# An opening by quarters, a rope ahead of a sum, and matmuls that nobody reads

## The chip, the core and the metric

The kernel runs on one core of one Trainium2 chip. The metric is the device time of one execution in microseconds (us), the median of several runs. Weights stream from HBM into SBUF by DMA, TensorE multiplies, VectorE (DVE), ScalarE (ACT) and GpSimd (POOL) do the rest, and SyncE (SP) issues nearly all transfers.

## The reference

Two layers, 256 tokens, 1024 features, everything in float32. Each layer mixes tokens (attention with 8 heads in one block of 256, beside a pooling mixer) and then applies a mixture of 16 experts, of which each token uses two. `plain` below is a layer norm without gain and bias, `LN` one with them.

```
cond = silu(c)
for l in 0, 1:
    sh1, sc1, g1, sh2, sc2, g2 = split(cond @ w_mod[l] + b_mod[l], 6)
    h = plain(x) * (1 + sc1) + sh1
    q, k, v, p = split(h @ w_in[l])               # 512 columns each
    a = attention(rope(q), rope(k), v)            # causal, softmax
    m = pool_mixer(p) @ w_pool[l] * pool_scale[l]
    x = LN1(alpha * x + g1 * (concat(a, m) @ w_out[l]))
    h = plain(x) * (1 + sc2) + sh2
    gates = top2_of_one_group(softmax(h @ w_router))
    y = sum_e gates[e] * (silu(h @ w_gate[e]) * (h @ w_up[e])) @ w_down[e]
    x = LN2(alpha * x + g2 * y)
```

## The kernel before

**The stream.** All weights, 265 MiB, come through one list of transfers, mostly of 1 MiB, in the order in which they are needed (`Stream`). SP issues the next one as soon as fewer than `limit` tiles are live; a tile is freed in the code behind its last matmul or VectorE operation, and the transfer that takes over its slot waits for that. The ring has 21 slots, some of which also serve as scratch; `st.allow` changes the limit between the stages.

**The order of the work.** Each engine runs its instructions in the order in which the code emits them, so a wait holds all that is emitted behind it on that engine. Nothing is reordered by a planner.

**The opening (layer 0).** `load_x` brings x in two halves of 128 tokens. `add_mod01(h)` lists the modulation weights of shift and scale for half h of the features (512): four tiles with rows of 512 columns, which are runs of 2 KB. `mod01(h)` multiplies them by the condition, `mod01_fin(h)` transposes the resulting row into columns and adds the bias. `enter` transposes the normalised x (L416) and applies scale and shift on its way to `hT`; `qk_mm` multiplies `hT` by the weights of queries and keys (L434), by feature blocks, for 128 tokens t at a time. The order is: half 0 of the features, its query and key matmuls for both t, half 1, its matmuls.

**The mixer.** `mod_dve(l, v, acc)` computes a modulation row on VectorE as a running sum of eight multiplies (L356, L358): v = 2 is the gate g1, 4 the scale sc2, 3 the shift sh2. `rope` turns queries and keys in place by twelve small VectorE operations (L709 to L714). `qT` and `kT` are transposes of them (L501), copied out by VectorE (queries) and ScalarE (keys) at L502; L508 and L513 are the scores. `pool` runs on GpSimd (L718 to L727). Before the change `mod_dve(l, 2)` stands ahead of `rope` in both layers.

**The router and the gather.** `exps`, `gate` and `router` rank the experts by a chain of small VectorE operations that ends in the mask `r_M`; five tiny matmuls with triangular and all-one matrices count the tokens of each expert (L784 to L789); `onehot` compares the result with slot numbers (L821), and `gather` copies the tokens into expert slots by matmuls with those one-hot matrices (L843).

**The experts.** Eight pairs a layer, each pair side by side in the halves of the array: `gate_up` (L885), `silu` (L899 to L902), `act_t` (four transposes, L908, and a copy, L910), `down` (L922), `combine` (L947). In layer 0 `mod_fin(1, 1)` stands behind the first pair's gate and up matmuls.

**Between the layers and at the end.** The last pair's results stay in PSUM. `experts` returns mean and power of the variance for both halves of the tokens, and the norms are applied by `norm` at the start of the next layer or at the end of the kernel, where `norm_aside` puts one quarter of it on ScalarE and GpSimd.

Of the kernel before, what the change touches and what calls it, by code (L numbers as in the profile page):

```python
# [16 lines left out]
D = 1024  # L17
# [56 lines left out]
def tile_trunk(ctx, tc, x, c, w_mod, b_mod, w_in, w_pool, pool_scale, w_out, ln1_g, ln1_b,  # L74
# [30 lines left out]
    def add_mod01(h):  # L105

        w = w_mod[0].rearrange("(p k) n -> p k n", k=8)
        for q in range(2):
            for v in range(2):
                st.add(("m01", h, q, v), w[:, 4 * q:4 * q + 4, v * D + h * 512:v * D + (h + 1) * 512])  # L110
# [42 lines left out]
    for h in range(2):  # L153
        add_mod01(h)
        if not h:
            load_x(1)
        add_qk(0, 2 * h)
        add_qk(0, 2 * h + 1)
# [46 lines left out]
    small_loads()  # L205
# [38 lines left out]

    pscol = const.tile([128, 8], F, name="pscol")
# [34 lines left out]

    colt = {}
# [31 lines left out]

    def mod01_fin(h, acc):
        part = s2()
        A.copy(part, acc)
        b = ps()
        for k in range(4):
            T.transpose(b[:, k * 128:(k + 1) * 128], part[:, k * 128:(k + 1) * 128], ident)
        o = col01[:, :, 4 * h:4 * h + 4]  # L320
        V.reduce_sum(o, b.rearrange("p (k v o r) -> p v k o r", k=4, v=2, o=2)[:, :, :, :, 0], axis=AX.X)
        V.tensor_add(o, o, bcol[:, 0, 4 * h:4 * h + 4, 0:2].rearrange("p k v -> p v k"))
# [58 lines left out]
    def stats_end(b):  # L381
        mv = tiny.tile([128, 2], F, name="mv")
        V.bn_aggr(mv, b)
        rs = tiny.tile([128, 1], F, name="rs")
# [25 lines left out]
    def enter(l, t, hT, xn, hs=(0, 1)):  # L410

        for h in hs:
# [12 lines left out]
    def mixer(l, hT, xn, ready):  # L425
        pq = [[ps(), ps()] for _ in range(2)]

        def qk_mm(t, qs=range(4)):
            for q in qs:
                w = st.get(("in", l, "qk", q))  # L430
                for kk in range(2):
# [4 lines left out]
                if t:  # L436
# [6 lines left out]
        else:  # L443

            ready(0)
            for t in range(2):
                qk_mm(t, (0, 1))
            ready(1)
            qk_mm(0, (2, 3))
        st.allow(NS - 6)  # L450
        qk = big.tile([128, 2, D], F, name="xn")
        for t in range(2):
            if t:
                qk_mm(1, range(4) if l else (2, 3))
# [6 lines left out]
        mod_dve(l, 2, acc[2])  # L461
        if l:
            mod_dve(l, 4, acc[4])
        rope(qk)

# [226 lines left out]
        exps(0)  # L692

# [50 lines left out]
    def router(l, mes, gate):  # L744
# [4 lines left out]
        gate()  # L749
# [409 lines left out]
```

## Time and profile before

| what | value |
|---|---|
| runs | 731.86 us median of 3 (729.12 to 734.01) |
| profiled execution | 732.26 us; span from first to last instruction 730.5 us |
| mean granted TensorE clock | 0.977 of full |
| busy share of the span | TensorE 92%, VectorE 44%, ScalarE 17%, GpSimd 6% |
| moved by DMA | 280.36 MB, mean 384 GB/s |

How to read it: busy time is the union of an engine's instructions over the span. The granted clock has two levels, 1.2 and 2.4 GHz; 0.5 in a window means the lower one throughout. The profile's rows name a line of the kernel and what it writes and reads: `ps` is a PSUM bank, `wr` a slot of the ring, `s` a scratch tile of 512 columns.

### The profile page before, as it was taken

How to read it: one execution, taken by the hardware profiler on the slowest of the kernel's cores; microseconds unless marked ns; L12 is line 12 of the kernel's file. 1: busy time of each engine (PE TensorE's matmuls, PEld its weight loads, DVE VectorE, ACT ScalarE, POOL GpSimd, SP SyncE). 2: the span in 40 equal slices, each digit the busy share in tenths (PEclk: the TensorE clock that was granted, in tenths of full speed). 3: DMA queues.
4: the chain of work that ended last, by engine and by line, in shares of the span. 5: the costliest groups of instructions: out<-in, count | busy, mean ns of one | idle time of the engine just before them, and what ended most of it. 6: DMA issues, size and time to landing. Idle time of an engine off the chain costs nothing. (4 is left out here: it accounts for less than half of the span.)

```text
span 730.5 us, 8092 instructions
## 1 busy us (share of the span) xinstructions
PE 675.4 (92%) x3101; PEld 322.0 (44%) x3101; DVE 323.9 (44%) x572; ACT 127.7 (17%) x274; POOL 46.9 (6%) x74
## 2 busy tenths in 40 slices
PE   4899799979899999999979999997999999998994
PEld 1347455544333363333324575555434345332331
DVE  2117898652243343232253876665332342342315
ACT  0111332122001121101102125213210111111100
POOL 4000500100000000000000041010000000000001
PEclk9999899999999999999999999997999999999998
DMA  9999999798999999999999999967599999999992
GB/s 325 395 391 408 410 370 379 282 415 323 423 422 419 421 421 423 421 417 418 398 408 390 409 410 415 372 266 309 216 423 421 422 421 421 421 418 421 418 399 91
DMA packets 57633, 280.36 MB, mean 384 GB/s; under 512 B 5009, under 2 KB 6073, under 8 KB 34537
## 3 DMA queue, kind: packets, MB, share of 16 engines
q1 hardware_dynamic: 56944, 279.20, 94.8%
q8 instruction: 29, 0.48, 0.3%
q10 hardware_dynamic: 312, 0.32, 0.1%
q0 software_dynamic: 320, 0.14, 0.1%
q14 instruction: 28, 0.22, 0.1%
HBM read 278.59 MB, written 1.05 MB: 383 GB/s over the span
## 5 line engine op out<-in xcount | busy, mean ns | idle before, releaser
L885 PE MATMUL ps<-wr 128*64 128x512 f32 x1024 | 224.3, 593 | 0.0
L885 PEld LDWEIGHTS ps<-wr 128*64 128x64 f32 x1024 | 73.1, 137 | 145.6 <-issue 140.7
L922 PE MATMUL ps<-wr,s 128*64 128x512 f32 x512 | 115.3, 602 | 4.0 <-ACT s L910 4.0
L922 PEld LDWEIGHTS ps<-wr,s 128*64 128x64 f32 x512 | 36.1, 138 | 73.3 <-issue 64.0
L932 DVE SCALAR_TENSOR_TENSOR s<-ps,gc,gb 128x512 f32<-128x512 f32 x32 | 23.9, 748 | 89.0 <-PE ps L922 89.0
L434 PE MATMUL ps<-wr,hT 128*128 128x512 f32 x128 | 56.9, 603 | 0.9 <-ACT hT L423 0.6
L596 PE MATMUL ps<-wr,hT 128*128 128x512 f32 (+1 forms) x160 | 55.7, 507 | 0.0
L358 DVE SCALAR_TENSOR_TENSOR wr<-wr,condT 128x1024 f32<-128x1024 f32 x42 | 54.2, 1290 | 2.3 <-DMA wr<-in_w_mod_dram 0.8
L935 ACT CAST wr<-s 128x512 fp32r<-128x512 f32 x30 | 18.5, 618 | 167.1 <-PE ps L885 109.1
L902 DVE TENSOR_TENSOR s<-s,ps 128x512 f32<-128x512 f32 x16 | 11.0, 687 | 79.4 <-PE ps L885 79.4
L936 DVE TENSOR_TENSOR wr<-s,wr 128x512 fp32r<-128x512 f32 x30 | 20.8, 692 | 55.6 <-ACT wr L935 50.8
L596 PEld LDWEIGHTS ps<-wr,hT 128*128 128x128 f32 x160 | 30.2, 190 | 23.8 <-issue 21.3
L434 PEld LDWEIGHTS ps<-wr,hT 128*128 128x128 f32 x128 | 24.4, 194 | 31.0 <-issue 28.5
L947 PE MATMUL ps<-wr,sT 128*128 128x512 f32 x120 | 33.6, 412 | 0.0
L910 ACT COPY s<-ps 128x512 f32<-128x512 f32 x16 | 9.4, 587 | 135.4 <-PE ps L908 135.4
L843 PE MATMUL ps<-s,xn 128*128 128x512 f32 x64 | 28.9, 451 | 2.1 <-DVE s L821 2.1
L1085 POOL TENSOR_TENSOR rs<-rs,mhalf 128x2 f32<-128x2 f32 x2 | 1.4, 702 | 457.1 <-DVE rs L1084 457.1
L552 PE MATMUL ps<-wr,hT 128*128 128x512 f32 x64 | 28.3, 596 | 0.0
L947 PEld LDWEIGHTS ps<-wr,sT 128*128 128x128 f32 x120 | 20.9, 189 | 16.3 <-issue 13.0
L478 PE MATMUL ps<-hT,wr 128*128 128x256 f32 x128 | 28.1, 380 | 0.0
L843 PE MATMUL ps<-s,hT 128*128 128x512 f32 x64 | 27.6, 431 | 0.0
L478 PEld LDWEIGHTS ps<-hT,wr 128*128 128x128 f32 x128 | 24.2, 190 | 4.5 <-issue 1.3
(236 smaller groups left out, 627.2 us busy)
## 6 DMA issues: line engine op xcount, KB each, us to landing
wr<-in_w_gate_dram SPq DMA_DIRECT2D x64, 1024.0 KB, 18.2
wr<-in_w_up_dram SPq DMA_DIRECT2D x60, 1024.0 KB, 18.8
wr<-in_w_down_dram SPq DMA_DIRECT2D x56, 1024.0 KB, 18.7
wr<-in_w_mod_dram SPq DMA_DIRECT2D x48, 1024.0 KB, 14.6
wr<-in_w_in_dram SPq DMA_DIRECT2D x16, 1024.0 KB, 16.7
wr<-in_w_out_dram SPq DMA_DIRECT2D x8, 1024.0 KB, 18.6
wr<-in_w_down_dram SPq DMA_DIRECT2D x12, 512.0 KB, 11.1
wr<-in_w_up_dram SPq DMA_DIRECT2D x8, 512.0 KB, 17.4
```

Of the source, the lines that this page charges most:

```text
L358: V.scalar_tensor_tensor(acc, w[:, kk], condT[:, k, 0:1], acc, op0=OP.mult, op1=OP.add)
L434: T.matmul(pq[t][n], hT[:, k, t * 128:(t + 1) * 128], w[:, kk, n * 512:(n + 1) * 512], start=(k == 0), stop=(k == 7))
L478: T.matmul(pp[g // 2][:, (g % 2) * 256:(g % 2) * 256 + 256], w[:, kk, g * 128:(g + 1) * 128], hT[:, k, :], start=(k == 0 and g % 2 == 0), ...
L552: T.matmul(pv[t], hT[:, k, t * 128:(t + 1) * 128], w[:, kk, :], start=(k == 0), stop=(k == 7))
L596: T.matmul(py[t][-1][:, 0:c1 - c0], catT[:, k, t * 128:(t + 1) * 128], w[:, kk, n * 512 + c0:n * 512 + c1], start=(q == 2 and kk == 0), st ...
L843: T.matmul(b, xs[:, t, k::8], SX[i][t], start=(n == 0), stop=(n == 3))
L885: T.matmul(bs[nm][64 * j:64 * j + 64, :], XE[i][k // 4][:, k % 4, c0:c0 + 64], st.get((nm, l, 2 * i + j, q))[:, k - k0, :], start=(k == 0) ...
L922: T.matmul(bo[n][64 * j:64 * j + 64, :], AT[i][:, k, 64 * j:64 * j + 64], st.get(("d", l, 2 * i + j, q))[:, k - k0, (n - n0) * 512:(n - n0 ...
L932: V.scalar_tensor_tensor(o, bo[n], GC[i], g2[:, c0], op0=OP.mult, op1=OP.mult)
L935: A.copy(oh[:, c0], o)
L936: V.tensor_sub(ol[:, c0], o, oh[:, c0].bitcast(F))
L947: T.matmul(b, STt[i][:, t * 128:(t + 1) * 128], o[:, n * 512:(n + 1) * 512], start=(start and j == 0), stop=(stop and j == 1), skip_group_ ...
```

## The change

- The opening goes by quarters of 256 features: two modulation tiles each (shift and scale, rows of 256 columns, runs of 1 KB), then one tile of query and key weights. `mod01`, `mod01_fin` and the new `enter01` handle a quarter; while a quarter's row is being turned into columns, TensorE multiplies the previous quarter's remaining blocks.
- The small loads on GpSimd's queue are issued behind the constants.
- In layer 0 the rope comes ahead of `mod_dve(0, 2)`.
- `warm(n)` multiplies an all-one matrix n times into a PSUM bank that nobody reads: 10, 2 and 3 times in the opening, 3 and 8 at the start of layer 1, 7 behind the first `exps` of layer 1, 6 behind `gate` and 4 behind the counts in both layers.
- `mod_fin(1, 1)` moves from expert pair 0 to pair 1 of layer 0; `act_t` splits its copy between VectorE and ScalarE in the first and last pair.
- The statistics of the second half of the tokens move behind the first half's norm work (`ends(t)`); three buffers instead of two for mean and power.

```diff
-        for q in range(2):
-            for v in range(2):
-                st.add(("m01", h, q, v), w[:, 4 * q:4 * q + 4, v * D + h * 512:v * D + (h + 1) * 512])
+        for v in (1, 0):
+            st.add(("m01", h, v), w[:, :, v * D + h * 256:v * D + (h + 1) * 256])
...
-    for h in range(2):
+    for h in range(4):
         add_mod01(h)
         if not h:
             load_x(1)
-        add_qk(0, 2 * h)
-        add_qk(0, 2 * h + 1)
+        add_qk(0, h)
...
     V.tensor_mul(condT[:, :, 0], th, cc)
-    small_loads()
     wr = const.tile([128, 8, 32], F, name="wr_")
...
     V.reciprocal(rcnt, rcnt)
 
+    small_loads()
...
+    def warm(n):
+
+        b = ps().rearrange("p (a c) -> p a c", a=4)
+        for _ in range(n):
+            T.matmul(b, ones, ones[:, None, :].to_broadcast([128, 4, 128]), start=True, stop=True)
...
     def mod01(h):
 
         acc = ps()
-        for q in range(2):
-            for kk in range(4):
-                for v in range(2):
-                    j = 2 * v + kk % 2
-                    T.matmul(acc[32 * j:32 * j + 32, :], condT[:, 4 * q + kk, :], st.get(("m01", h, q, v))[:, kk, :],
-                             start=(q == 0 and kk < 2), stop=(q == 1 and kk > 1))
+        for k in range(8):
             for v in range(2):
-                st.free(("m01", h, q, v))
-        return acc
-
-    def mod01_fin(h, acc):
-        part = s2()
-        A.copy(part, acc)
+                j = 2 * v + k % 2
+                T.matmul(acc[32 * j:32 * j + 32, 0:256], condT[:, k, :], st.get(("m01", h, v))[:, k, :],
+                         start=(k < 2), stop=(k > 5))
+        for v in range(2):
+            st.free(("m01", h, v))
+        part = s2(256)
+        A.copy(part, acc[:, 0:256])
+        return part
...
-        mv = tiny.tile([128, 2], F, name="mv")
+        mv = tiny.tile([128, 2], F, name="mv", bufs=3)
...
+    def enter01(h, hT, xn):
+
+        b = ps()
+        for k in range(2):
+            for t in range(2):
+                T.transpose(b[:, k * S + t * 128:k * S + (t + 1) * 128],
+                            xn[:, t, (2 * h + k) * 128:(2 * h + k + 1) * 128], ident)
+        return b
+
+    def enter01_fin(h, hT, b):
+        for k in range(2):
+            kk = 2 * h + k
+            o, i = hT[:, kk, :], b[:, k * S:(k + 1) * S]
+            if k:
+                V.tensor_scalar(o, i, colt[0, 1][:, kk:kk + 1], colt[0, 0][:, kk:kk + 1], op0=OP.mult, op1=OP.add)
+            else:
+                A.activation(o, i, AF.Identity, scale=colt[0, 1][:, kk:kk + 1], bias=colt[0, 0][:, kk:kk + 1])
...
-            ready(0)
-            for t in range(2):
-                qk_mm(t, (0, 1))
-            ready(1)
-            qk_mm(0, (2, 3))
+            for q in range(4):
+                if not q:
+                    ready(0)()
+                qk_mm(0, (q,))
+                if q < 3:
+                    fin = ready(q + 1, lambda: qk_mm(1, (q,), (0,)))
+                    qk_mm(1, (q,), (1,))
+                    fin()
...
-        mod_dve(l, 2, acc[2])
         if l:
+            mod_dve(l, 2, acc[2])
             mod_dve(l, 4, acc[4])
         rope(qk)
+        if not l:
+            mod_dve(l, 2, acc[2])
...
         exps(0)
+        if l + 1 == DEPTH:
+            warm(7)
...
         gate()
+        warm(6)
...
         T.matmul(pc[:, 0:16], ones, M[:, 1], start=False, stop=True)
+        warm(4)
...
-            A.copy(a, b.rearrange("p (k s) -> p k s", k=4))
+            bv = b.rearrange("p (k s) -> p k s", k=4)
+            if i in (0, NPAIR - 1):
+                V.tensor_copy(a[:, 0:2], bv[:, 0:2])
+                A.copy(a[:, 2:4], bv[:, 2:4])
+            else:
+                A.copy(a, bv)
...
-                    V.bn_stats(bn[t][:, 1, :], XB[t][1])
...
-                if l + 1 < DEPTH:
-                    mod_fin(l + 1, 1)
...
+            if i == 1 and l + 1 < DEPTH:
+                mod_fin(l + 1, 1)
...
-        mv2 = tiny.tile([128, 2, 2], F, name="mv2", bufs=1)
-        rs2 = tiny.tile([128, 2], F, name="rs2", bufs=1)
-        for t in range(2):
-            V.bn_aggr(mv2[:, t], bn[t])
-        V.tensor_scalar_add(rs2, mv2[:, :, 1], EPS)
-        P.tensor_tensor(rs2, rs2, mhalf.to_broadcast([128, 2]), op=OP.pow)
-        return [(mv2[:, t], rs2[:, t:t + 1]) for t in range(2)], norm, norm_aside
+        def ends(t):
+            V.bn_stats(bn[t][:, 1, :], XB[t][1])
+            return stats_end(bn[t])
+
+        return ends, norm, norm_aside
...
+            warm(10)
             bias_cols()
 
-            def ready(h):
-                mod01_fin(h, mod01(h))
-                for t in range(2):
-                    enter(0, t, hT, xn, (h,))
+            def ready(h, between=lambda: None):
+                part = mod01(h)
+                if not h:
+                    warm(2)
+                between()
+                mod01_fin(h, part)
+                b = enter01(h, hT, xn)
+                if not h:
+                    warm(3)
+                return lambda: enter01_fin(h, hT, b)
         else:
             mod_mm(l, 0)
+            warm(3)
...
                 b = tiny.tile([128, 2, 6], F, name="bn")
+                if not t:
+                    own.append(ends(0))
...
-                V.tensor_scalar(xn[:, t], xt[:, t], mv[:, 0:1], rs, op0=OP.subtract, op1=OP.mult)
                 if not t:
                     mod_fin(l, 0)
+                    warm(8)
+                    own.append(ends(1))
+                V.tensor_scalar(xn[:, t], xt[:, t], mv[:, 0:1], rs, op0=OP.subtract, op1=OP.mult)
                 enter(l, t, hT, xn)
...
+    def second():
+        own[1] = ends(1)
+        norm_aside(1, 512, D, rest, *own[1])
```

## Rows read from the trace of the kernel before

In the windows the columns are: stretch, its length, busy time and instructions of the engines, the granted clock, DMA share, GB/s. In a timeline they are: start, duration, engine, line, operation, tiles, count, and in brackets the idle time before and what ended it.

**Rows 1.** Windows: DMA rate in five stretches.
```profile
41.00:50.00 9.00, 8.41 (x28) 4.44 (x29) 1.86 (x7) 2.46 (x6) 0.00 (x0) 1.00 1.05 380
250.00:300.00 50.00, 50.00 (x232) 24.12 (x230) 16.88 (x27) 6.13 (x9) 0.00 (x0) 1.00 1.01 421
90.00:180.00 90.00, 84.80 (x440) 47.76 (x440) 59.43 (x101) 25.16 (x52) 5.15 (x5) 0.98 0.89 353
470.00:522.00 52.00, 47.62 (x271) 29.81 (x271) 31.51 (x71) 13.84 (x26) 4.08 (x4) 0.90 0.62 243
522.00:716.00 194.00, 189.11 (x874) 76.07 (x871) 60.38 (x101) 23.82 (x39) 0.00 (x0) 1.00 1.00 413
```

**Rows 2.** Waits of TensorE: us in total, times, longest.
```profile
PE ps L501 <- DVE xn L714: 5.7, 2, 4.2
...
PE ps L908 <- DVE s L902: 3.6, 4, 1.8
PE ps L784 <- DVE r_M L778: 2.8, 2, 2.3
PE ps L843 <- DVE s L821: 2.1, 2, 1.0
PE ps L624 <- DVE wr L391: 1.9, 1, 1.9
...
PE ps L293 <- DMA wr<-in_w_mod_dram: 1.2, 1, 1.2
```

**Rows 3.** Timeline of the opening.
```profile
18.16 1.28 DVE L378 BATCH_NORM_STATS2 bn<-xt 128x6 f32<-128x512 f32 x2 [3.31 <-DMA xt<-in_x_dram]
...
23.14 14.00 PE L434 MATMUL ps<-wr,hT 128*128 128x512 f32 x32 [0.65 <-ACT hT L423]
...
37.07 3.64 PE L308 MATMUL ps<-wr,condT 128*32 128x512 f32 x32
...
41.94 1.04 PE L416 MATMUL ps<-ident,xn 128*128 128x128 f32 x8
...
43.12 14.00 PE L434 MATMUL ps<-wr,hT 128*128 128x512 f32 x32
```

**Rows 4.** Timeline from the gate's sum to the scores, layer 0.
```profile
62.98 9.21 DVE L358 SCALAR_TENSOR_TENSOR wr<-wr,condT 128x1024 f32<-128x1024 f32 x7
...
73.47 2.11 POOL L718 TENSOR_TENSOR wr<-wr 128x1084 f32<-128x1084 f32 x1 [1.03 <-DMA wr<-in_w_mod_dram]
...
73.64 2.08 DVE L710 TENSOR_TENSOR s<-xn,cs 128x128 f32<-128x128 f32 x1
...
80.83 2.08 PE L508 MATMUL ps<-wr 64*128 64x128 f32 x16
```

**Rows 5.** Timeline of the tail, VectorE.
```profile
721.47 0.74 DVE L1067 SCALAR_TENSOR_TENSOR xt<-ps,mv,wr 128x512 f32<-128x512 f32 x1
```

**Rows 6.** Windows: stretches at the lower clock.
```profile
76.20:83.00 6.80, 4.04 (x26) 3.75 (x28) 3.87 (x5) 0.59 (x1) 6.39 (x12) 0.50 1.03 410
158.20:161.60 3.40, 3.40 (x8) 2.80 (x9) 0.36 (x1) 0.78 (x1) 0.00 (x0) 0.51 1.00 422
...
383.40:386.80 3.40, 3.40 (x11) 2.27 (x11) 3.29 (x6) 2.52 (x8) 0.00 (x0) 0.50 1.03 408
496.10:502.90 6.80, 6.22 (x29) 2.96 (x28) 4.97 (x15) 2.49 (x6) 0.00 (x0) 0.50 1.01 418
506.30:509.70 3.40, 3.40 (x9) 2.81 (x9) 0.81 (x1) 0.78 (x1) 0.00 (x0) 0.50 0.18 75
```

**Rows 7.** Timeline of layer 1's router, VectorE.
```profile
499.61 0.17 DVE L684 TENSOR_REDUCE r_mx<-ps 128x1 f32<-128x16 f32 x1 [1.05 <-PE ps L683]
```

**Rows 8.** Timeline of the passage to layer 1.
```profile
375.56 0.70 DVE L943 BATCH_NORM_STATS2 bnx<-ps 128x6 f32<-128x512 f32 x1 [0.16 <-PE ps L942]
...
381.20 0.66 PE L332 MATMUL ps<-ident,s 128*128 128x128 f32 x4 [0.71 <-ACT s L327]
...
382.33 0.81 DVE L1112 TENSOR_SCALAR xn<-xt,mv,rs 128x1024 f32<-128x1024 f32 x1 [0.73 <-POOL rs L386]
```

More of the change, by code (lines that the diff above doesn't have):

```diff
@@ L303, in mod01, with mod01_fin @@
         acc = ps()
-        for q in range(2):
-            for kk in range(4):
-                for v in range(2):
-                    j = 2 * v + kk % 2
-                    T.matmul(acc[32 * j:32 * j + 32, :], condT[:, 4 * q + kk, :], st.get(("m01", h, q, v))[:, kk, :],
-                             start=(q == 0 and kk < 2), stop=(q == 1 and kk > 1))
-            for v in range(2):
-                st.free(("m01", h, q, v))
-        return acc
-    def mod01_fin(h, acc):
-        part = s2()
-        A.copy(part, acc)
+        for k in range(8):
+            for v in range(2):
+                j = 2 * v + k % 2
[6 more added lines that the diff above has]
+        return part
+    def mod01_fin(h, part):
         b = ps()
-        for k in range(4):
+        for k in range(2):
             T.transpose(b[:, k * 128:(k + 1) * 128], part[:, k * 128:(k + 1) * 128], ident)
-        o = col01[:, :, 4 * h:4 * h + 4]
-        V.reduce_sum(o, b.rearrange("p (k v o r) -> p v k o r", k=4, v=2, o=2)[:, :, :, :, 0], axis=AX.X)
-        V.tensor_add(o, o, bcol[:, 0, 4 * h:4 * h + 4, 0:2].rearrange("p k v -> p v k"))
+        o = col01[:, :, 2 * h:2 * h + 2]
+        V.reduce_sum(o, b[:, 0:256].rearrange("p (k v o r) -> p v k o r", k=2, v=2, o=2)[:, :, :, :, 0], axis=AX.X)
+        V.tensor_add(o, o, bcol[:, 0, 2 * h:2 * h + 2, 0:2].rearrange("p k v -> p v k"))
     def mod_fin(l, v):
@@ L381, in stats_end @@
     def stats_end(b):
-        mv = tiny.tile([128, 2], F, name="mv")
+        mv = tiny.tile([128, 2], F, name="mv", bufs=3)
         V.bn_aggr(mv, b)
-        rs = tiny.tile([128, 1], F, name="rs")
+        rs = tiny.tile([128, 1], F, name="rs", bufs=3)
         V.tensor_scalar_add(rs, mv[:, 1:2], EPS)
@@ L407, in norm_rows, with enter @@
         return ts
-    def enter(l, t, hT, xn, hs=(0, 1)):
-        for h in hs:
+    def enter01(h, hT, xn):
[6 more added lines that the diff above has]
+    def enter01_fin(h, hT, b):
+        for k in range(2):
+            kk = 2 * h + k
[4 more added lines that the diff above has]
+                A.activation(o, i, AF.Identity, scale=colt[0, 1][:, kk:kk + 1], bias=colt[0, 0][:, kk:kk + 1])
+    def enter(l, t, hT, xn):
+        for h in range(2):
             b = ps()
@@ L426, in mixer, with qk_mm @@
         pq = [[ps(), ps()] for _ in range(2)]
-        def qk_mm(t, qs=range(4)):
+        def qk_mm(t, qs=range(4), kks=range(2)):
             for q in qs:
                 w = st.get(("in", l, "qk", q))
-                for kk in range(2):
+                for kk in kks:
                     for n in range(2):
@@ L435, in qk_mm @@
                                  start=(k == 0), stop=(k == 7))
-                if t:
+                if t and 1 in kks:
                     st.free(("in", l, "qk", q))
@@ L453, in mixer @@
             if t:
-                qk_mm(1, range(4) if l else (2, 3))
+                qk_mm(1, range(4) if l else (3,))
             A.activation(qk[:, t, 0:512], pq[t][0], AF.Copy, scale=DH ** -0.5)
@@ L1119, in tile_trunk @@
     rest = xt[:, 1, 512:D]
+    own = [ends(0), None]
+    def second():
+        own[1] = ends(1)
+        norm_aside(1, 512, D, rest, *own[1])
     for t, a, b in ((0, 0, 512), (0, 512, D), (1, 0, 512)):
-        norm(t, a, b, xt[:, t, a:b], *ends[t], (lambda: norm_aside(1, 512, D, rest, *ends[1])) if t == a == 0 else None)
+        norm(t, a, b, xt[:, t, a:b], *own[t], second if t == a == 0 else None)
         nc.sync.dma_start(out[0, t * 128:(t + 1) * 128, a:b], xt[:, t, a:b])
```

3 lines of the change are left out of this document (2 added, 1 removed).

## The prediction

> **What bounds the kernel now.** I read first the windows of DMA traffic by stage, then who waited for whom on TensorE, then the windows where the granted clock falls, and last the timelines of the places that the change touches. All times are of the profiled execution, 732.26 us with a span of 730.5; the median of the three runs, 731.86, lies 0.4 lower.
>
> The weight stream and TensorE bound this kernel in turns, tied by the ring of slots. The reader is to see this in [rows 1]. With 8 KB runs and no gap the stream moves 421 GB/s (stretch 250 to 300). From 90 to 180 it moves 353, so (421 - 353) / 421 x 90 = 14.5 us of it are lost, because slots come free only as the mixer, the router and the first expert pair use their weights. From 470 to 522 it moves 243: 22 us lost in the same way in layer 1. From 522 to 716 it runs at 413 almost unbroken while TensorE is busy 189 of 194 us; TensorE starts those experts with a full ring and ends with an empty one. So what TensorE saves inside the expert pairs is taken back by the stream, seen at the end of layer 0 as the 1.2 us that L293 waits for its last modulation tile [rows 2]. What TensorE and VectorE save ahead of the first expert pair lets slots go, and the stream run, earlier by as much, up to the lost time of that layer. I therefore count savings ahead of 167 us (layer 0) and between 380 and 515 us (layer 1), and the tail, and nothing else.
>
> **The change part by part.**
>
> *Opening.* The queries' and keys' matmuls start at 23.14, 4.98 after the second half of x arrives at 18.16 [rows 3]. Ahead of it stood x's first half and four tiles (4.2 MB) of modulation weights; now two (2.1 MB), which at 380 GB/s [rows 1] is 5.5 us sooner. The tiles now have rows of 1 KB, which no row here shows. Per engine of the 16, a 2 KB packet takes 2048 x 16 / 380 = 86 ns and an 8 KB one 8192 x 16 / 421 = 311 ns, so 37 ns per KB and 12 ns for each packet; 1 KB would take 49 ns, 334 GB/s (estimate), 0.4 us more per tile. The bounds are no loss (86 / 2 = 43 ns) and a packet that costs 86 ns whatever its size (190 GB/s); I take 49, for the line passes through both sizes. So the start moves to 23.14 - 5.5 + 0.8 = 18.4. From there TensorE does 28.0 of query and key matmuls (two times 14.00), three modulation quarters at half of 3.64 (5.5), and three times six transposes at 1.04 / 8 (2.3) [rows 3]: 35.8, ending at 54.2 where it ended at 57.1. The copy and reduction behind each quarter lie under 1.75 us of matmuls that the change places between them; without that cover they would cost 1 us a quarter, the bound on this side. A quarter's 3.15 MB take 8.9 us of stream against 9.6 of TensorE, so data just keep up. Gain 3.0, between 0 and 5. The ten first filling matmuls, the small loads moved on GpSimd's queue behind the constants, and the bias transposes lie ahead of x's arrival: nothing, as long as GpSimd's nine issues, now ahead of the statistics' power, end before x's second half is in; if not, some 1 us. The third buffer of the statistics costs nothing.
>
> *Rope ahead of the gate's modulation sum (layer 0).* TensorE waits 5.7 us in two waits for the rope [rows 2]. It stands behind the sum's eight multiplies, which run to 62.98 + 9.21 = 72.19; of its twelve operations the first seven take 1.5 us, up to 73.64, and the next was held up for 2.08 beside GpSimd's addition [rows 4]. Now the rope runs before GpSimd starts, in some 2.7 us, and the sum ends at 74.9 in the old time. Its four slots come free 2.7 later, and the three matmuls of the gate's rows that need it stay behind it; the ring is not short of slots before 90. The wait is not gone: the query copies on VectorE now stand behind the sum, and the score matmuls behind them. With a copy like the 0.74 of a 128x512 operation [rows 5] they start at 75.6 where they started at 80.83: 5.2. If the last multiply (9.21 / 7 = 1.3) must wait for the addition that ends at 73.47 + 2.11 = 75.58 [rows 4], they start at 77.6: 3.2. In addition the clock ran at half speed from 76.2 to 83.0, with TensorE busy 4.04 [rows 6], so up to 2.0 come back if the shorter wait leaves it high. I take 5.0 for the whole, between 3.2 and 7.1.
>
> *Filling matmuls in the routers.* Each has 512 columns in one pass, as a gather's matmul has, of which eight took 3.40 at half clock: 0.43, or 0.21 at full [rows 6]. Layer 0 has six in a wait of 2.3 and four in one of 1.05, layer 1 seven in 1.9, six and four [rows 2]; at full clock 1.3, 0.9 and 1.5, so they fit and cost nothing; at half clock they would overrun by 0.3, 0.7 and 1.1. In layer 1 the six stand in a wait of only 0.5, but the stretch before it ran at half clock and shortens. What they can give is the clock. The gathers' first 3.4 us ran at half speed in both layers, after TensorE had stood idle on VectorE's ranks: 1.7 each. In layer 1 it was at half speed from 496.1 to 502.9 too, after the 1.9 us wait: there VectorE waited 1.05 for the second logits [rows 7] and would start that much sooner. 1.7 in layer 0 and 2.7 in layer 1, and a loss of 1 in each layer if the clock falls all the same.
>
> *Between the layers.* Of the statistics, one bn_stats (0.70) and an aggregation leave the way to the first half. But the second half's now stand between the shift's reduction and the normalisation xn, which ended at 383.14. The reduction waits for transposes of the modulation row, which end at 381.86; some 0.4 for it, 0.70 and two small operations (0.3) for the statistics, and 0.81 for xn make 384.1 [rows 8]: 1.0 later. The eleven fills lie in that wait; they may save the half clock from 383.4 to 386.8 (1.7, [rows 6]). I take 0, between -1.0 and +0.7.
>
> *Within the experts.* Moving the mod_fin from pair 0 to pair 1 and halving act_t's copy shorten the 3.6 us of waits at L908 [rows 2] and the copies behind them; at pair 1 TensorE then waits some 1.2 for the moved copy, which stands behind act_t's on ScalarE. All of it is spent against the stream: 0 (the moved accumulator holds a PSUM bank longer, also 0).
>
> *Tail.* The second half's statistics now follow the first normalisation operation (0.74, [rows 5]), less one aggregation: 0.6 later.
>
> Sum: 3.0 + 5.0 + 1.7 = 9.7 in layer 0, under the stream's 14.5 - 3.0 (eight tiles x 0.4) = 11.5; 0 between the layers; 2.7 in layer 1, far under 22; -0.6: 11.8. From 732.26 that is 720.5, on the median's scale 720.
>
> **Rivals.**
>
> *The clock falls all the same.* Then 1.7, 2.7 and the rope's 1 to 2 are missing: 731.9 - (3.0 + 4.0 - 0.6) = 725.5. For it: the fills are short and much around them in the routers are transposes and matmuls of 32 columns. Against it: the waits that they fill are just those after which it fell. The Trainium skill, "TensorE: Matmul & The Clock Gate", section "Part 4: PE-mode transpose", says that transposes don't lift the clock, since they do not count as busy in the same way; no row here separates them, and by it this rival is what happens in layer 1's router, where sixteen follow the fills.
>
> *The rope's wait comes back whole.* If GpSimd's additions (2.11 and those after) get in between VectorE's last two multiplies, the scores start at 79 or later and only 1 is left: 731.9 - (3.0 + 1.0 + 1.7 + 2.7 - 0.6) = 724. The held-up operation of 2.08 beside an addition of 2.11 speaks for it [rows 4]; that seven of the eight multiplies end before the addition starts speaks against it. The Trainium skill, "VectorE: DVE Perf Modes", section "Two Vector instructions with no wait between them", calls the interface through which VectorE reads a second SBUF operand shared with GpSimd; the multiply, too, reads two, and by that rule the 3.2 above is the price and not the 5.2.
>
> *Slower: the 1 KB packets bound the opening.* If a packet costs 86 ns whatever its size, two tiles take 11 us, a quarter 13.7, and the last quarter's matmuls end near 72 where they ended at 57: 15 lost, of which 8.8 come back later (5.0 + 1.7 + 2.7 - 0.6), so 738. It decides below about 300 GB/s, where a quarter's data take longer than its TensorE work, and turns the whole slower at about 220. The rates at 2 and 8 KB speak against it, for there the price follows the size.
>
> *More is set free.* The opening gives 5, the rope 7.1, and layer 0 reaches the stream's 11.5: with 2.7 and 0.7 that is 717.5.
>
> **How the numbers follow.** The forecast 0.53, the clock 0.19, the rope 0.13, more 0.09, slower 0.06. The range goes from 717.5 less the runs' own spread (2.7 below the median) to the clock rival with the low opening and rope, 731.9 - (0 + 3.2 - 0.6) = 729.3: 715 to 729. Faster by over 1% means below 724.5, and 1% (7.3 us) is about what a measurement of runs from 729.12 to 734.01 tells from none: the forecast, "more", half of the rope's and a little of the clock's, 0.73. Within 1%: 0.21. Slower: 0.06.
>
> **What would show it.** Right: scores' first matmul near 73 instead of 80.83; query and key matmuls from 18 to 54; full clock in both gathers; 353 and 243 GB/s both higher; L293's wait for its tile kept or longer; VectorE's chain at the end longer by 0.6. Wrong: TensorE waiting for DMA inside the opening, fills that delay the matmul behind them, VectorE's multiplies of the sum over 1.3 us beside GpSimd, or an expert stage of layer 1 that does not end earlier though it starts earlier.

## The result, and the profile after

The changed kernel takes 724.39 us, median of eight runs (721.74 to 726.67), beside 731.44 for the kernel before: a ratio of 0.990 (95% interval 0.9875 to 0.9924), a gain of 7.05 us where 11.8 were forecast. Measured a second time it took 724.16 beside 733.32: 0.9885 (0.9860 to 0.9911). Its profiled execution took 721.74 with a span of 719.9, 10.5 under the span of before. It happens to be the fastest of the eight: its mean granted clock was 0.991, that of the other seven 0.986 to 0.989. So the next paragraphs compare two single executions, and what separates them from the medians is a question for the experiments.

The stretches of the execution, as windows (columns as in [rows 1]):

```profile
22.00:55.00 33.00, 32.99 (x173) 15.50 (x173) 2.77 (x10) 5.24 (x11) 0.00 (x0) 1.00 1.06 376
85.00:175.00 90.00, 87.33 (x460) 48.83 (x460) 59.49 (x101) 23.18 (x47) 5.21 (x5) 1.00 0.99 400
460.00:511.00 51.00, 48.25 (x297) 30.37 (x298) 32.55 (x72) 14.37 (x27) 4.14 (x4) 1.00 0.67 262
511.00:705.00 194.00, 188.62 (x873) 76.40 (x870) 61.16 (x103) 23.38 (x39) 0.00 (x0) 1.00 1.00 413
...
75.60:79.00 3.40, 3.40 (x20) 2.77 (x16) 3.04 (x6) 1.64 (x10) 3.24 (x7) 0.50 1.03 408
151.50:155.00 3.50, 3.43 (x13) 3.46 (x14) 1.33 (x2) 0.82 (x2) 0.00 (x0) 1.00 1.02 431
321.30:324.70 3.40, 3.40 (x10) 0.98 (x8) 0.69 (x1) 1.80 (x4) 0.00 (x0) 0.50 1.02 410
...
495.60:499.00 3.40, 3.33 (x13) 3.36 (x14) 1.33 (x2) 0.78 (x1) 0.00 (x0) 1.00 0.67 282
```

Beside [rows 1] the stream from the scores to the first expert pair rose from 353 to 400 GB/s, that of layer 1's router from 243 to 262, and the expert stage of layer 1 is what it was: 413 over 194 us. Beside [rows 6] both gathers (151.5 and 495.6) now run at the full clock. What is left at the lower one, up to the last matmuls, is one stretch at the scores, and one inside layer 0's experts, now at 321.3.

The places that the change touches, as a timeline (columns as in [rows 3]):

```profile
16.67 0.55 PE L418 MATMUL ps<-ident,xn 128*128 128x128 f32 x3 [1.37 <-DVE xn L394]
18.06 3.70 PE L455 MATMUL ps<-wr,hT 128*128 128x512 f32 x8 [0.20 <-ACT hT L429]
22.01 1.29 PE L311 MATMUL ps<-wr,condT 128*32 128x256 f32 x20 [0.25 <-DMA wr<-in_w_mod_dram]
...
54.20 0.22 PE L260 MATMUL ps<-ident,s 8*128 8x8 f32 x1
...
63.03 10.82 DVE L361 SCALAR_TENSOR_TENSOR wr<-wr,condT 128x1024 f32<-128x1024 f32 x7
70.61 2.15 POOL L746 TENSOR_TENSOR wr<-wr 128x1084 f32<-128x1084 f32 x1 [1.03 <-ACT wr L513]
74.60 1.22 PE L534 MATMUL ps<-wr 64*128 64x128 f32 x16 [3.48 <-DVE wr L528]
...
87.84 9.21 DVE L361 SCALAR_TENSOR_TENSOR wr<-wr,condT 128x1024 f32<-128x1024 f32 x7
97.69 1.04 PE L372 MATMUL ps<-ident,wr 128*128 128x128 f32 x8
...
371.00 1.06 PE L297 MATMUL ps<-wr,condT 128*32 128x512 f32 x8 [0.86 <-DMA wr<-in_w_mod_dram]
372.77 0.66 PE L335 MATMUL ps<-ident,s 128*128 128x128 f32 x4
374.80 0.80 DVE L1159 TENSOR_SCALAR xn<-xt,mv,rs 128x1024 f32<-128x1024 f32 x1
375.66 1.09 PE L437 MATMUL ps<-ident,xn 128*128 128x128 f32 x8 [0.51 <-DVE xn L1159]
376.87 14.00 PE L455 MATMUL ps<-wr,hT 128*128 128x512 f32 x32
```

and, for the last of these, the queries and keys of layer 1 in the kernel before:

```profile
384.89 14.90 PE L434 MATMUL ps<-wr,hT 128*128 128x512 f32 x32
```

The opening does what was forecast: query and key matmuls from 18.06 (forecast 18.4) to 54.20 (54.2), with one wait of 0.25 for a transfer. The seven multiplies of the gate's sum, which now meet GpSimd's first addition at 70.61, take 10.82 where the same seven alone take 9.21 (L361 at 87.84, and [rows 4]). So at least one of them took well over 1.3 beside GpSimd, which is one of the prediction's own signs of being wrong. The scores start at 74.60, behind a wait of 3.48, where the prediction had them near 73. VectorE's second sum ends at 87.84 + 9.21 = 97.05, and the transposes that need it (L372) start at 97.69 without a wait.

The table shows where the 10.5 between the two executions lie, by the starts of the same TensorE matmuls in both timelines (before 107.10, 167.59, 379.42, 384.89, 514.98; after 100.57, 159.74, 371.00, 376.87, 503.86; the line numbers are those of the kernel after):

| from, to | before | after | gained |
|---|---|---|---|
| start to output projection of layer 0 (L622) | 107.10 | 100.57 | 6.5 |
| to the first expert pair (gather in it) | 60.49 | 59.17 | 1.3 |
| to the last modulation tile ahead of layer 1 (L297) | 211.83 | 211.26 | 0.6 |
| to layer 1's queries and keys | 5.47 | 5.87 | -0.4 |
| to layer 1's first expert pair | 130.09 | 126.99 | 3.1 |
| to the end of the span | 215.5 | 216.1 | -0.6 |

### The profile page after: what moved, and what is told of

Its sections match the earlier page's. It is cut to its first block, busy times and chain, and to the rows that moved or that the text cites. A ratio compares the mean times of both kernels' runs of the same rounds, so it can differ in the third digit from the quotient of the medians.

```text
span 719.9 us, 8334 instructions
## 1 busy us (share of the span) xinstructions
PE 678.6 (94%) x3213; PEld 324.8 (45%) x3218; DVE 325.4 (45%) x582; ACT 124.8 (17%) x268; POOL 49.7 (7%) x76
## 3 DMA queue, kind: packets, MB, share of 16 engines
HBM read 278.59 MB, written 1.05 MB: 388 GB/s over the span
## 5 line engine op out<-in xcount | busy, mean ns | idle before, releaser
L957 PE MATMUL ps<-wr,s 128*64 128x512 f32 x512 | 113.7, 595 | 3.7 <-DVE s L942 2.9
L957 PEld LDWEIGHTS ps<-wr,s 128*64 128x64 f32 x512 | 35.6, 137 | 71.9 <-issue 63.4
L455 PE MATMUL ps<-wr,hT 128*128 128x512 f32 x128 | 57.0, 597 | 0.4 <-ACT hT L429 0.2
L361 DVE SCALAR_TENSOR_TENSOR wr<-wr,condT 128x1024 f32<-128x1024 f32 x42 | 55.8, 1329 | 2.3 <-DMA wr<-in_w_mod_dram 0.8
L622 PE MATMUL ps<-wr,hT 128*128 128x512 f32 (+1 forms) x160 | 55.7, 507 | 0.1
L389 POOL TENSOR_TENSOR rs<-rs,mhalf 128x1 f32<-128x1 f32 x16 | 13.2, 824 | 551.2 <-DVE rs L388 551.2
L622 PEld LDWEIGHTS ps<-wr,hT 128*128 128x128 f32 x160 | 30.2, 190 | 23.8 <-issue 21.5
L455 PEld LDWEIGHTS ps<-wr,hT 128*128 128x128 f32 x128 | 23.6, 190 | 28.9 <-issue 27.3
L873 PE MATMUL ps<-s,xn 128*128 128x512 f32 x64 | 27.2, 425 | 0.3 <-DVE s L851 0.3
L930 DVE SCALAR_TENSOR_TENSOR s<-s,ps 128x512 f32<-128x512 f32 x16 | 11.0, 685 | 36.4 <-ACT s L929 36.4
L873 PE MATMUL ps<-s,hT 128*128 128x512 f32 x64 | 25.9, 405 | 0.0
```

Of the source, the lines that this page charges most:

```text
L361: V.scalar_tensor_tensor(acc, w[:, kk], condT[:, k, 0:1], acc, op0=OP.mult, op1=OP.add)
L455: T.matmul(pq[t][n], hT[:, k, t * 128:(t + 1) * 128], w[:, kk, n * 512:(n + 1) * 512], start=(k == 0), stop=(k == 7))
L622: T.matmul(py[t][-1][:, 0:c1 - c0], catT[:, k, t * 128:(t + 1) * 128], w[:, kk, n * 512 + c0:n * 512 + c1], start=(q == 2 and kk == 0), st ...
L873: T.matmul(b, xs[:, t, k::8], SX[i][t], start=(n == 0), stop=(n == 3))
L957: T.matmul(bo[n][64 * j:64 * j + 64, :], AT[i][:, k, 64 * j:64 * j + 64], st.get(("d", l, 2 * i + j, q))[:, k - k0, (n - n0) * 512:(n - n0 ...
```

## The experiments

Each edit is one to the changed kernel. The first four were timed beside each other, then the next four, then the last four; where the changed kernel is not in a group, its two medians, 724.39 and 724.16, stand for it. The kernel before was timed in each group, with medians of 733.32, 732.79 and 732.13, so a difference of about 1 us between groups may be drift. Each paragraph begins with the median and the range of the runs.

**The changed kernel again.**

> The changed kernel once more, nothing altered. The question is why its profiled execution stands 10.5 us under that of the kernel before (721.7 against 732.3) while the medians stand 7.0 apart. Theory one (chance of the execution): the profiled execution of the change was its fastest by luck, with fewer half-clock stretches; then this profile falls anywhere from 720 to 725 in span, the new median is again 724.4 (723.5 to 725.5), and a longer span shows half-clock stretches or a slower stream at places where the first profile had none. Rival (the profile itself reads low for the change): the new profiled execution is again within 1 us of 721.7 while the timed median stays near 724.4.

724.16 (723.28 to 726.42). This profiled execution was the slowest of its six, 726.42 with a span of 724.5. So the first profile was low by the chance of its execution, and the trace says where. Windows of that execution:

```profile
18.20:21.60 3.40, 3.40 (x7) 1.32 (x5) 0.71 (x2) 0.56 (x1) 0.00 (x0) 0.51 1.11 368
...
373.20:376.60 3.40, 3.32 (x12) 0.92 (x13) 0.00 (x0) 0.59 (x1) 0.47 (x1) 0.50 1.00 401
...
666.80:670.20 3.40, 3.40 (x9) 0.92 (x9) 0.69 (x1) 2.56 (x5) 0.00 (x0) 0.50 1.01 412
```

and its timeline at the ends of the waits ahead of them:

```profile
17.68 0.55 PE L418 MATMUL ps<-ident,xn 128*128 128x128 f32 x3 [1.84 <-DVE xn L394]
...
161.97 13.95 PE L915 MATMUL ps<-wr 128*64 128x512 f32 x64
...
370.69 1.06 PE L297 MATMUL ps<-wr,condT 128*32 128x512 f32 x8 [1.01 <-DMA wr<-in_w_mod_dram]
373.28 1.93 PE L297 MATMUL ps<-wr,condT 128*32 128x512 f32 x8 [1.52 <-DMA wr<-in_w_mod_dram]
...
666.40 1.54 PE L408 MATMUL ps<-rowz,selz 128*128 128x512 bf16 x4 [2.13 <-PEq L1055]
```

There are three half-clock stretches that the first profile doesn't have, each at a wait of 1.5 to 2.1 us that the change didn't fill: for x, for the weights of the last modulation tile, and at a branch of the program (PEq is TensorE's sequencer). The 4.6 between the two spans divide as follows: queries start 1.1 later (x arrives later), from there to the first pair 1.1 (142.80 against 141.68; the stretch at 18.2), at the passage 1.4 (L297 to L455 in 7.28 against 5.87), in layer 1's experts 0.9 (217.0 against 216.1). And one thing that cost nothing: the first execution ran at half clock from 321.3 to 324.7 and this one didn't, yet from the first pair to the last modulation tile both take the same, 211.26 and 211.31. What TensorE lost there the first execution got back by waiting less for that tile's weights: 0.86, against 1.01 + 1.52 here.

**Without the fills.**

```diff
     def warm(n):
+        return
```

> The filling matmuls are left out everywhere (they write a bank that nobody reads); all else is as in the change. By my terms they are worth 1.7 in layer 0's gather and 2.2 to 2.7 in layer 1's router and gather, so the time goes from 724.4 to 728.3 to 728.8, and the half-clock stretches at both gathers (3.4 us each) and at the passage between the layers come back. Rival one: the clock would have stayed up without them, since the waits became shorter by the other edits: 724.4, no half-clock stretch at the gathers. Rival two: only layer 1's counts on the median, because layer 0's savings are taken back by the stream: 726.6.

728.49 (727.17 to 729.25), 4.3 slower than the changed kernel beside it. Windows of this run:

```profile
19.90:23.30 3.40, 3.40 (x5) 1.34 (x5) 0.28 (x1) 0.00 (x0) 0.00 (x0) 0.50 1.06 385
...
156.40:159.80 3.40, 3.40 (x10) 2.76 (x10) 0.81 (x1) 0.98 (x2) 0.00 (x0) 0.50 1.02 429
381.70:385.10 3.40, 3.40 (x4) 1.49 (x5) 3.23 (x7) 2.37 (x7) 0.00 (x0) 0.50 1.02 395
494.30:501.10 6.80, 5.91 (x23) 2.30 (x24) 5.21 (x19) 1.94 (x6) 0.00 (x0) 0.50 1.01 423
```

The half-clock stretches of [rows 6] are back at layer 0's gather, at the passage and in layer 1's router. Both rivals fall. That 4.3 is so near my two terms, 4.4, is in part luck, for the edit takes out the fills of the opening and of the passage as well. The two places that the terms are for show 1.5 (from layer 0's gather to its first pair 9.63 instead of 8.17) and 2.0 (from layer 1's queries to its first pair 129.02 instead of 126.98): 3.5. The other 0.8 would belong to the opening, with the stretch at 19.9, and to the passage, where executions differ by more than that.

**The rope behind the sum again.**

```diff
+        mod_dve(l, 2, acc[2])
         if l:
-            mod_dve(l, 2, acc[2])
             mod_dve(l, 4, acc[4])
         rope(qk)
-        if not l:
-            mod_dve(l, 2, acc[2])
```

> Layer 0's rope stands behind the gate's modulation sum again, as in the kernel before; all else is as in the change. By the term of my prediction this costs 5.0: 729.4. By the trace of the changed kernel, where the score matmuls came 3.4 sooner and the value matmuls 2.7, it costs 2.7: 727.1. Rival (layer 0 has reached what the stream gives, so that this saving had been taken back): within 1 of 724.4, and the wait for the modulation tile between the layers is shorter instead.

727.66 (725.24 to 730.00): it is 3.5 slower than the changed kernel beside it, between my two numbers. Its timeline:

```profile
72.80 1.61 DVE L738 TENSOR_TENSOR s<-xn,cs 128x128 f32<-128x128 f32 x1
...
77.77 1.89 PE L532 MATMUL ps<-wr 64*128 64x128 f32 x16
...
100.90 1.13 PE L372 MATMUL ps<-ident,wr 128*128 128x128 f32 x8 [0.83 <-DVE wr L361]
```

One of the rope's operations, which take 0.28 in the changed kernel, is held to 1.61 beside GpSimd again. The scores come 3.2 later than in the changed kernel (77.77 against 74.60), the shift's transposes (L372) as well (100.90 against 97.69), and there TensorE waits for VectorE's second sum.

**The opening by halves again.** The opening's hunks of the diff are reversed: four tiles of 512 columns, two `ready`, `small_loads` in its old place.

> The opening by halves of 512 features, with 2 KB rows, and the small loads' issues where they stood before; all else is as in the change (the filling matmuls within the opening, behind the tenth, are gone with it). By my term and by the shift of the last query and key matmul in the traces (57.05 to 54.20) it costs 2.9: 727.3. Rival (the stream takes it back by the end of layer 0): 724.4 to 725.5, though the opening itself ends 2.9 later.

727.11 (725.39 to 727.45): it is 2.95 slower than the changed kernel beside it, as forecast. By the medians nothing of it is taken back on the way to the end. What the quarters, the small loads and the two fills each give of it is not separated.

**The expert pairs as before.**

```diff
-            if i in (0, NPAIR - 1):
+            if False:
...
+                if l + 1 < DEPTH:
+                    mod_fin(l + 1, 1)
             silu(i)
...
-            if i == 1 and l + 1 < DEPTH:
-                mod_fin(l + 1, 1)
```

> The modulation reduction that the change moved from expert pair 0 to pair 1 stands at pair 0 again, and the copies behind the activations' transposes of the first and last pair lie on ScalarE alone again; all else is as in the change. My term: what TensorE saves inside the expert pairs is taken back by the stream, so nothing: 724.4, within 1, with waits of TensorE at these pairs some 1.5 to 3 longer and the wait for the modulation tile at the end of layer 0 shorter. Rival (these waits lie on the path): 1.5 to 3 slower, 726 to 727.5.

723.62 (723.12 to 724.94): nothing is lost, though part of the waits are back. Waits of TensorE in this run:

```profile
PE ps L957 <- ACT s L945: 4.0, 8, 0.7
...
PE ps L938 <- DVE s L932: 3.6, 4, 1.8
...
PE ps L297 <- DMA wr<-in_w_mod_dram: 1.7, 2, 1.5
```

In the changed kernel it waits 2.1 at L938 and 3.8 in all at L957. The wait at L297, which I expected shorter, is longer here, 1.7 against 0.9; in the repeated execution of the changed kernel it was 2.5, so one trace doesn't decide that sign.

**The tail in another order.**

```diff
         own[1] = ends(1)
-        norm_aside(1, 512, D, rest, *own[1])
...
     norm(t, a, b, ..., second if t == a == 0 else None)
+    if t == a == 0:
+        norm_aside(1, 512, D, rest, *own[1])
```

> At the very end the second half's ScalarE and GpSimd path is asked for behind the whole first normalisation instead of between its two operations; all else is as in the change. In the changed kernel VectorE's second operation of the first normalisation waits from 710.1 to 711.9 for GpSimd's power of the other half. If that is the 0.65 that the tail lost, VectorE's chain and the first output leave 0.7 sooner and the end comes 0.3 to 0.6 sooner: 723.9. Rival (the path over ScalarE and GpSimd sets the end): no change, 724.4.

724.59 (722.09 to 725.28): there is no gain, and from L977 to the end it took 12.9 instead of 12.7. VectorE's second operation did move ahead (713.32, 1.0 behind the first one's end instead of 1.8), but it then runs beside GpSimd's power for the other half. Rows of GpSimd and VectorE in this run:

```profile
713.55 0.92 POOL L389 TENSOR_TENSOR rs<-rs,mhalf 128x1 f32<-128x1 f32 x1 [1.15 <-DVE rs L388]
715.55 1.69 POOL L1111 TENSOR_TENSOR xt<-xt,wr 128x512 f32<-128x512 f32 x1 [1.08 <-ACT xt L1110]
716.81 0.97 DVE L1104 SCALAR_TENSOR_TENSOR xt<-xt,rs,wr 128x512 f32<-128x512 f32 x1
717.31 1.59 POOL L1112 TENSOR_TENSOR xt<-xt,wr 128x512 f32<-128x512 f32 x1
```

and VectorE's last one in the changed kernel:

```profile
715.41 0.97 DVE L1104 SCALAR_TENSOR_TENSOR xt<-xt,rs,wr 128x512 f32<-128x512 f32 x1
```

In the changed kernel GpSimd's first two took 0.55 and 1.26, its last one ended at 715.83, and VectorE ended last, at 716.38. So there VectorE's chain sets the end, and not the path over ScalarE and GpSimd as the rival has it. In the new order VectorE ends 0.9 sooner, counted from the start of L977 (8.3 against 9.1), but GpSimd 0.8 later (9.4 against 8.6), and now sets the end: the rival's time came true, for another reason.

**The gate's sum split.**

```diff
-            mod_dve(l, 2, acc[2])
+            mod_dve(l, 2, acc[2], range(3))
...
+        if not l:
+            mod_dve(l, 2, acc[2], (3,))
         b0 = [ps(), ps()]
```

`range(3)` are the first three of the sum's four tiles, with two multiplies each.

> Layer 0's gate sum is split: six of its eight multiplies ahead of the query copies on VectorE, two behind them. All else is as in the change. If the score matmuls wait for the sum's last multiplies, which GpSimd's first addition held up by 1.6, they start at 72.4 instead of 74.6, and the clock may stay high there. What is late next is the shift's own sum on VectorE, which ends at 97.05 whatever TensorE does; its transposes stand in TensorE's order 0.6 behind that, so of the 2.2 to 3.7 only 0.6 is left: 723.8. Rival (VectorE's chain doesn't bind, the stream has room): 2.2 to 3.7 faster, 720.7 to 722.2. Second rival (the stream takes it back): 724.4.

725.27 (721.93 to 726.27): the scores start sooner, and by the median nothing comes of it. Its timeline:

```profile
72.71 1.16 PE L535 MATMUL ps<-wr 64*128 64x128 f32 x16
72.99 4.35 DVE L361 SCALAR_TENSOR_TENSOR wr<-wr,condT 128x1024 f32<-128x1024 f32 x2
...
98.37 1.32 PE L372 MATMUL ps<-ident,wr 128*128 128x128 f32 x8 [2.92 <-DVE wr L361]
```

and a window behind that wait:

```profile
99.20:102.60 3.40, 3.40 (x22) 2.11 (x22) 3.33 (x5) 0.59 (x1) 1.06 (x1) 0.50 1.03 411
```

The wait of 3.48 is gone from the scores, and one of 2.92 stands at the shift's transposes. The two multiplies behind the copies take 4.35 where two alone take 2.6: GpSimd's price of 1.6 to 1.7 is paid wherever they stand. In this execution the clock stayed up at the scores and fell behind the new wait instead: from L372 to the output projection it took 4.54 instead of 2.88, 1.7 more, which is over the 0.6 that was left to gain. The fastest two of the six runs, 721.93 and 723.57, had clocks of 0.993 and 0.991, the other four 0.986 to 0.989; whether the 0.6 stays where the clock does is not shown.

**The split, and the shift's transposes later.** In addition to the last edit:

```diff
             mod_dve_fin(l, 2, acc[2])
-            mod_dve_fin(l, 4, acc[4])
+            if l:
+                mod_dve_fin(l, 4, acc[4])
...
-        sc2, g1 = colt[l, 4], gb[l, 2]
+        g1 = gb[l, 2]
+        if not l:
+            out_mm(0)
+            mod_dve_fin(l, 4, acc[4])
+        sc2 = colt[l, 4]
...
-        out_mm(0)
+        if l:
+            out_mm(0)
```

> The same split, and the shift's transposes and reduction stand behind the first half of the output projection, so that TensorE doesn't wait for VectorE's sum. If that sum is what binds, this gives the rest: 2.2 for the earlier scores, up to 1.5 for the clock there: 720.7 to 722.2. Rival (the stream binds layer 0 by now): the wait for the modulation tile at the end of layer 0 grows from 0.9 by as much as layer 0's attention saves, and the time is 723.5 to 724.4.

722.48 (721.22 to 722.85): that is 2.8 under the split alone, and 1.7 to 1.9 under the changed kernel, a little less than the theory's 2.2 to 3.7. In its timeline the matmuls that stood behind L372 go on at 95.28:

```profile
72.60 1.16 PE L536 MATMUL ps<-wr 64*128 64x128 f32 x16
...
95.28 1.09 PE L603 MATMUL ps<-wr 128*64 128x128 f32 x16
```

**The shift's transposes later, without the split.** The second edit of the last experiment alone.

> Only the second half of the split2 experiment: the shift's transposes and reduction stand behind the first half of the output projection, the gate sum is not split. All else is as in the change. Theory (two things stand in a row in layer 0, the score wait and VectorE's chain up to the shift's sum, and each alone hides the other): TensorE reaches these transposes at 97.5, just as VectorE's sum ends (97.05), so moving them saves nothing: within 0.7 of 724.3. Rival (the moved reduction alone made split2 faster, because VectorE starts the next sum 1.7 sooner): 722.5.

724.66 (723.74 to 726.02), which is no gain. In its timeline the scores still wait for the sum:

```profile
76.86 2.08 PE L535 MATMUL ps<-wr 64*128 64x128 f32 x16 [3.48 <-DVE wr L529]
```

By the medians both edits together give 1.7 to 1.9, and neither alone gives anything: there are two waits in a row, each of which hides the other. A part of the 2.8 between the split alone and both is the clock, which fell behind the second wait.

**xn ahead of the second half's statistics, between the layers.**

```diff
                     mod_fin(l, 0)
-                    warm(8)
+                    warm(4)
+                V.tensor_scalar(xn[:, t], ...)
+                if not t:
                     own.append(ends(1))
-                V.tensor_scalar(xn[:, t], ...)
```

> Between the layers, the normalisation xn of the first half stands ahead of the second half's statistics on VectorE, and four instead of eight filling matmuls behind the shift's transposes; all else is as in the change. In the changed kernel xn starts at 374.80, 1.04 behind the reduction's end, and the transposes wait for it until 375.66. Theory (this wait lies on the path): xn starts at 373.8, the transposes 0.7 to 1.0 sooner, and as the stream is not the bound from there to the end of layer 1's router, all of it stays: 723.4 to 723.7. Rival (the second half's statistics are late instead and their tile's query and key matmuls wait): 724.3.

723.36 (721.09 to 725.50): its median is 0.8 to 1.0 under the changed kernel's, which the runs don't tell from drift between the groups, so the trace carries it:

```profile
374.20 0.66 PE L335 MATMUL ps<-ident,s 128*128 128x128 f32 x4
...
376.05 1.09 PE L437 MATMUL ps<-ident,xn 128*128 128x128 f32 x8 [0.33 <-DVE xn L1158]
...
377.25 4.99 PE L455 MATMUL ps<-wr,hT 128*128 128x512 f32 x11
```

From the row's transposes (L335) to the queries and keys (L455) it is 3.05, in the changed kernel 372.77 to 376.87, 4.10, so 1.05 are gained there.

**Six more fills in the opening.**

```diff
                 mod01_fin(h, part)
+                if not h:
+                    warm(6)
                 b = enter01(h, hT, xn)
```

> Six more filling matmuls in the opening, between the first modulation transposes and the transposes of x, where TensorE waits 1.4 to 1.85 for x's second half; all else is as in the change. Theory (where x arrives late, TensorE stands idle over 1.8 and the clock falls at 17.7 to 18.2 for 3.4, which costs 1.3 and stays to the end): the half-clock stretch near 18 is gone in every execution, and the median falls by up to 1.3, more than the lowest time: 723.0 to 723.9. Rival (the loss is taken back by the stream in layer 0, or the fills overrun x's arrival): 724.3 or more.

722.90 (722.35 to 724.04): the median falls by 1.3 to 1.5, and the highest run (724.04) lies below the changed kernel's median. By the ratios to the kernel before, each in its own group, it is only 0.5 (0.9878 against 0.9885), so the size stays open. The wait for x in its timeline is 0.28, and in this one trace no stretch near 18 is at the lower clock:

```profile
15.08 1.46 PE L283 MATMUL ps<-ones 128*128 128x512 bf16 x6
...
16.93 0.55 PE L418 MATMUL ps<-ident,xn 128*128 128x128 f32 x3 [0.28 <-DVE xn L394]
```

**Together.** split2, xn_first, open_fills and the tail's order.

> split2, xn_first, open_fills and the order of the tail experiment together; all else is as in the change. If they add up: 724.3 less 1.9 (split2), 0.7 to 1.0 (xn), up to 1.3 (opening), 0 to 0.4 (tail): 720.0 to 721.5. If the stream binds layer 0 after split2, the opening's part is lost: 721.5 to 722.

720.32 (718.59 to 722.02), ratio to the kernel before 0.9845 (0.9815 to 0.9875): this is the fastest version. The parts add up, by the medians (1.8 + 1.0 + 1.4 less 0.3 of the tail, against 3.9) as well as by the ratios to the kernel before (2.0 + 0.4 + 0.5, against 2.9). One of its windows:

```profile
85.00:175.00 90.00, 86.06 (x455) 47.42 (x457) 59.86 (x104) 23.13 (x46) 4.77 (x5) 1.00 1.02 415
```

415 GB/s from the scores on leave little that layer 0's mixer and router could still set free (421 in the experts).

## Why the prediction came out as it did

The direction, the places and most of the mechanisms held; the gain was put too high, 11.8 where the medians show 7 to 9. By the time alone that isn't shown: 724.4 lies nearer to two of the rivals (724 and 725.5) than to the forecast's 720, and it is the traces and the undoing of each part that speak against these.

*What bounds the kernel: held for layer 0.* Savings ahead of a layer's first expert pair reach the end, those inside layer 0's pairs don't. From the first pair to the last modulation tile the profiled executions of all these kernels take 211.2 to 212.6, with a half-clock stretch in between or without, and with the pairs' waits of before or of after. What TensorE gains there it waits out at L297 (0.86 against 2.53 in the two executions of the changed kernel). In layer 1 the same step is too strong: a half-clock stretch inside the experts costs 0.9 at the end, so there the stream takes back only a part.

*Opening: held.* 3.0 were forecast, 2.9 show in the trace and 2.95 by undoing it. Data just kept up, with one wait of 0.25. The estimate of 49 ns for a packet of 1 KB, against the rival's 86, is right: in the transfer records of the changed kernel's trace the median packet of 1 KB takes 49 ns, of 2 KB 88 and of 8 KB 311. The quarters, a mixture of these tiles and longer rows, ran at 364 to 376 GB/s. That rival is out.

*Rope: the step that was mis-sized.* I took 5.0, near the upper end of the scores' 5.2; it measured 3.5. Of the two prices that I gave for the scores, 3.2 was the right one (77.77 to 74.60), for the last multiplies do meet GpSimd's addition: 10.82 instead of 9.21. The Trainium skill, "VectorE: DVE Perf Modes", section "Two Vector instructions with no wait between them", calls the interface through which VectorE reads a second SBUF operand shared with GpSimd, and the trace agrees in so far as the multiplies, which read two, are slowed; that it is this interface no run separates. The up to 2.0 for the clock came only in part: one stretch of 3.4 at half speed was left where two had been, and in the traces of tail, experts_back and late_fin, which do the same up to there, both are left. And the step looked at the scores' wait alone: VectorE's chain up to the shift's sum ends only 0.6 before TensorE reaches that sum's transposes (97.05 against 97.69), so removing the scores' wait alone could give no more than that, as split, late_fin and split2 show together. The rope's move paid because it shortened both by the same 3.2. The rival in which only 1 is left falls.

*Fills: held, a little too high.* 1.7 and 2.7 were forecast. By leaving them out these places show 1.5 and 2.0, and in the two profiled executions 1.3 and 2.2 (the 3.1 of layer 1 less 0.9 of its queries and keys, 14.90 to 14.00, which is the passage's clock). The rival that the clock falls all the same is out: with transposes behind the fills layer 1's router and gather still ran at 1.00 throughout (460 to 511 in the windows after). The Trainium skill, "TensorE: Matmul & The Clock Gate", section "Part 4: PE-mode transpose", says that transposes don't lift the clock; that is not tested here, for the clock was up before them.

*Between the layers: both parts held, the sum about 0.* xn came 1.0 late as computed (1.05 by xn_first), and the clock gave 0.9 back in the profiled execution. In the repeated one a stretch at half clock came back there and cost 1.4.

*Experts 0 and tail -0.6: held.* Undoing the first loses nothing, and the second shows 0.6 in the table; from the last matmuls (L977) to the end it is 0.7, 12.7 instead of 12.0.

*What was missing.* By undoing, opening, rope and fills give 2.95 + 3.5 + 4.3 = 10.75; less 0.6 of the tail and 1.05 of the late xn that is 9.1. The two kernels timed beside these runs stood 733.32 - 724.16 = 9.2 apart; in the first measurement it was 7.05. Against the 11.8 of the sum the rope was 1.5 too high, the routers' fills 0.9, and the late xn is 1.05 that I had weighed against a clock gain; the fills of the opening and the passage, which the sum put at nothing, would make up for 0.8. The forecast was also made against one execution, and the changed kernel still loses the clock in some executions at waits that have no fill: for x (1.1 in the repeated one; with open_fills it didn't), for the last modulation tile (1.4) and for the branch in layer 1's experts (0.9). The profiled execution of after had none of the three. Whether the kernel before loses it there as often stays open, for I have one trace of it, without the last of them. Its 13 executions beside the repetition had mean clocks of 0.972 to 0.984, the changed kernel's six 0.985 to 0.993, so its profiled execution, at 0.977, was no outlier. What makes 7 in one measurement and 9 in the other stays open too.

## What to carry to other kernels

A wait that stands on one engine's way may hide another engine's chain right behind it, so before pricing its removal follow the next wait down the same path; only the two edits together paid here. Savings count where the stream is held up by slots that come free late, and little or not at all in a stage that the stream already fills. An experiment that takes out an edit everywhere prices all its places together; take the single ones from the trace. Compare several executions of the same kernel before crediting a difference of 1% to an edit: here two executions of one kernel stood 4.6 apart, about half of the change.

## What the runs showed of the hardware that was not expected

- The clock falls or stays up from execution to execution at the same wait. At the branch in layer 1's experts TensorE waited 1.92 to 2.34 in the 13 traces of the changed kernel and its variants, and the clock fell in six of them; at 2.13 it fell in the repeated run, and at 2.34 in the first it didn't.
- Behind a wait for x of 1.84 the clock fell (at 18.2 in the repeated run), behind one of 1.37 it didn't (first run).
- GpSimd's own operations are held as well when VectorE works beside them: the power of one column took 0.92 instead of 0.55, a multiply of 128x512 1.69 instead of 1.26, enough to undo what a better order on VectorE gave.
- Half clock for 3.4 us inside the experts cost nothing at the end of layer 0 (211.26 with it, 211.31 without), and 0.9 at the end of layer 1 (217.0 against 216.1).
